# One layer of S5, grouped-query attention and experts: the order of VectorE and ScalarE between the unit loop and the last stage's square root, by hand before, the scheduler's after

## The chip, the core and the metric

The kernel runs on one core of one Trainium2 chip. The metric is the device time of one execution in microseconds (us), launch to end. The core's engines are TensorE (PE; its weight loads are a row of their own, PEld), VectorE (DVE), ScalarE (ACT), GpSimd (POOL) and SyncE (SP), beside 16 DMA engines that carry all loads. Each engine works through its own list of instructions in order, and waits on semaphores for data of the others.

## What is computed

One layer of a hybrid backbone over 256 latent tokens and 256 context tokens of width 1024, in float32. The reference, cut to what matters here:

```python
h  = _modulate(_rmsnorm(x, norm1_g), sh1, sc1)            # latent tokens
hc = _modulate(_rmsnorm(ctx, norm1_g), sh1c, sc1c)        # context tokens
proj, proj_c = h @ w_in, hc @ w_in[:, :COL_Q]             # S5 input | K | V | Q | gates
y_ssm  = _s5_mixer(proj[:, :512], proj_c[:, :512], ...)   # bidirectional scan, 32 groups
o_attn = _attention(q, k_all, v_all)                      # 8 heads of 64, 512 keys
s = gelu(y_ssm); s = s * sigmoid(s @ w_glu + b_glu)
merged = gates[:1024] * (s @ w_ssm_out) + gates[1024:] * (o_attn @ w_attn_out)
x_mix  = x + g1 * (merged @ w_out)
h2 = _modulate(_rmsnorm(x_mix, norm2_g), sh2, sc2)
out = _rmsnorm(x_mix + g2 * _moe(h2, ...), final_norm_g)  # top 4 of 32 experts
```

The modulation vectors (sh1 to g2) are products of the conditioning vector with w_mod. An expert is act(x @ w_gate_up + b_gate_up) @ w_down + b_down, with a clamped SwiGLU. All 32 experts' weights, 12 MB each, are read once.

## The kernel before

SBUF is cut into 24 pages of 1 MB (128 partitions x 2048 floats). Weights come as whole pages through SyncE's queue, in an order written out in the program; a page that becomes free is handed to the next load by `release` (L168) or `used` (L189), and since SyncE's instructions stay in program order (`load`, L104), a load whose page is not free holds up all later loads. GpSimd issues a few small DMAs of its own.

The front of the program runs up to the end of the branches: modulation, normalisation, products with w_in for the S5 input, K, V and Q, tables for the S5 kernels (`v_tables`, `w_tables`), and then **the unit loop** (16 units, from L1203). In one unit stand: half a gate tile's product (`gate_mm`, from tile 2 on with weights split into a high and a low part, `gate_split`), in some units a modulation tile's product (`mod_tile`, eight matmuls of 512 columns), two S5 kernel groups (`k_kernel`, units 2 to 5), a few steps of the scan (`scan_some`), and one softmax block (`attn`: scores, maximum, exponential; two units later the transposes; every fourth the product with V). At fixed units: `q_T` and `k_T` (unit 2: transposes of q and k, copied out by both engines); write and reading back of the S5 kernel tables through a DRAM tile Rd by GpSimd (unit 5); `mod_rows` (unit 10: modulation rows 1 and 2, kept in page 3); `scan_out` (end of unit 10: the scan's states to page 8, four ACT and four DVE copies); `shift_logits` (unit 11: transposes of a modulation row, copied to shT, which a product for the router's constant uses); readout, gelu and glu in units 12 to 15. `bias_steps` casts the expert biases b_gate_up and b_down, in page 3's rows, into bf16 parts in page 7, ACT and DVE in turn; a step stands at places from unit 9 on.

Behind the loop `branch` (L1267) multiplies by w_ssm_out (four products of 24 matmuls) and w_attn_out (four more). Each splits the next piece of weights (`wsplit`: ACT copies the high part, DVE subtracts for the low part), takes up to four bias steps, and merges with the gate on DVE. Then come `warm(AF.Sqrt, ...)`, which loads the square root's table on ACT, the output product (`out_mm`, `out_add`), the router, and 32 experts, each of eight pages of w_gate_up and four of w_down.

What sets the order: `keep_in_program_order` pins an instruction among the pinned ones of its engine, and the scheduler places the others by its own reckoning. TensorE is pinned through `pinned`, SyncE always. VectorE and ScalarE are written as `V` and `S`, objects of the class `Pinned`, whose calls are all recorded at one line, L49, and which pin while `strict["vec"]` holds. Before, it holds from ahead of the first products with w_in to the end. GpSimd is not pinned.

In the order rows below, pg_N is page N - 60 (pg_63 is page 3), pg_1242 and pg_1243 are the high and low parts of split weights (pages 13 and 10), pg_308 and pg_309 those of activations, bk_N is a bank that TensorE writes, smx and ssum are the softmax's maximum and sum.

Of the kernel before, what the change touches and what calls it, by code (L numbers as in the profile page):

```python
# [33 lines left out]
def hybrid_block(ctx: ExitStack, tc: tile.TileContext, a: dict, out: bass.AP):  # L34
# [3 lines left out]
    strict = {"on": False, "vec": False}  # L38
# [35 lines left out]
    def sm(shape, name, dt=F32):  # L74
        return pool.tile(shape, dt, name=name)
# [30 lines left out]
    def load_g(dst, src):  # L106
        return G.dma_start(dst, src)
# [95 lines left out]
    def mod_tile(reload=True):  # L203
        i, k = divmod(mods["done"], 8)
        mods["done"] += 1
        if k == 0:
            mbk[i + 1] = bank(("mod", i + 1))
        p_ = where["mod", i, k]
        for q in range(4):
            mm(mbk[i + 1][32 * q:32 * q + 32], scond[:, k], pg(p_, 512 * q, 512), k == 0, k == 7)  # L210
        if reload:
            mod_load(p_)
        return p_
# [87 lines left out]
    def warm(func, src):  # L301
        pa_(S.activation(sm([128, 1], f"warm{state['warm']}"), src, func))
        state["warm"] += 1
# [519 lines left out]
    def rope_q():  # L823
        for t in range(2):
            qv = qn[:, t].rearrange("p (h f) -> p h f", h=8)
            rope_norm(qv, q_ps[t].rearrange("p (h f) -> p h f", h=8), cosq[:, t], sinq[:, t],
                      rsn[:, 8 * t:8 * t + 8], 8, qv)
            del held["q", t]
# [17 lines left out]
    def q_split():  # L846
        for t in range(2):
            split(qn[:, t].rearrange("p (h f) -> p h f", h=8), qs[:, t, :, 0], qs[:, t, :, 1], V)
# [63 lines left out]
    def scan_some(cols):  # L912
        while cols > 0:
            step = next(scan_left, None)
            if step is None:
                return
            cols -= step[1] + 2
# [41 lines left out]
    def gate_mm(i, j):  # L959
        if j == 0:  # L960
            gbk[0] = bank("g")
        for k in range(8):
            o = gbk[0][:, 256 * j:256 * j + 256]
            if i < N_WHOLE:
                mm(o, loaded["gate", i][:, k, 128 * j:128 * j + 128], hT[1][:, k], k == 0, k == 7)
            else:
                mm3(o, wg[0][:, j, k], wg[1][:, j, k], hH[:, k], hL[:, k], k == 0, k == 7)
        if i < N_WHOLE and j:
            used("gate", i)

        if j:
            S.activation(gtl[i // 4][:, 512 * (i % 4):512 * (i % 4) + 512], gbk[0], AF.Tanh, scale=0.5)
            del held["g"]
# [15 lines left out]
    def k_kernel(g8):  # L989

        g4, g1, e = g8 // 4, g8 % 4, g8 % 2
        if g1 == 0:
            kb[0], kb[1] = bank("kf"), bank("kb")
        bf, bb = kb[0], kb[1]
        bd = bf[:, 448:512]
        for kind in range(3):
            for r, W in ((0, WR), (1, WI)):
                for q in range(4):
                    g = 8 * q + g8
                    Wq = W[q][:, g8]  # L1000
                    st = BBf[:, r, (g - e) * 16:(g - e) * 16 + 32]
                    rows_ = slice(32 * q, 32 * q + 32)
                    if kind == 0:
                        mm(bf[rows_, 112 * g1:112 * g1 + 112], st[0:64], Wq[0:64, 0:7], r == 0, r == 1)
                    elif kind == 1:
                        mm(bb[rows_, 112 * g1:112 * g1 + 112], st[64:128], Wq[64:128, 1:8], r == 0, r == 1)
                    else:
                        mm(bd[rows_, 16 * g1:16 * g1 + 16], st, CT[:, r, g], r == 0, r == 1)
        if g1 == 3:
            gs = slice(4 * g4, 4 * g4 + 4)  # L1010
            S.activation(R[:, gs, 128:240], bf[:, 0:448].rearrange("p (g m) -> p g m", g=4), AF.Copy)
            S.activation(R[:, gs, 0:112], bb[:, 0:448].rearrange("p (g m) -> p g m", g=4), AF.Copy)
            V.tensor_add(R[:, gs, 112:128], bd.rearrange("p (g m) -> p g m", g=4), Dm[:, gs])
            del held["kf"], held["kb"]
# [68 lines left out]
    def attn_norm(c_i):  # L1083
        if 0 <= c_i < 16:
            score_norm(c_i)
# [109 lines left out]
    def next_split(u, part):  # L1195
        if 2 * N_WHOLE <= u < 16:
            gate_split(u // 2, u % 2, part)
            if part and u % 2:
                used("gate", u // 2)


    n_attn = 0
    for u in range(16):  # L1203
        next_split(u + 1, 0)
        attn_norm(n_attn - 1)
        next_split(u + 1, 1)
        if u > 2:
            scan_some(P_SC)
        gate_mm(u // 2, u % 2)
        if u < 3 or (u % 2 == 0 and mods["done"] < 16):  # L1210
            mod_tile(u > 1)
        if 2 <= u < 6:
            k_kernel(2 * u - 4)
            k_kernel(2 * u - 3)
        if u == 0:
            rope_q()
        if u == 1:
            rope_k()
            q_split()
            S.activation(hH.bitcast(F32R), hT[1], AF.Copy)  # L1220
        if u == P_QT:
            for i in range(2):
                q_T(i)
                k_T(i)
            V.tensor_sub(hL.bitcast(F32R), hT[1], hH)
        if u > 1:
            scan_some(P_SC)
        if u == 4:
            mod_bias()
        if u == 5:  # L1230
            Rd = dpool.tile([16, 32, 240], F32, name="Rd")
            for q in range(4):
                for e in range(2):
                    load_g(Rd[:, 8 * q:8 * q + 8].rearrange("p (g e) m -> p e g m", e=2)[:, e],
                           R[32 * q + 16 * e:32 * q + 16 * e + 16].rearrange("p (g e) m -> p e g m", e=2)[:, e])
            kernel_in()
        if u == P_M:
            mod_rows(1)
            mod_rows(2)
        if u == P_M + 1:  # L1240
            shift_logits()
        if u >= P_B:
            next(bias_left, None)
        if u >= P_A:
            attn(n_attn)
            n_attn += 1
        if u >= P_B:
            next(bias_left, None)
        if u == P_S:
            scan_some(1000)  # L1250
            scan_out()
        if u in (P_RO, P_RO + 1):
            readout(u - P_RO)
        if u == P_RO + 1:
            release(18, 19, 11, 12)
            load(n2row, w("norm2_g")[None, :].to_broadcast([128, 1024]))
        if u == P_RT:
            readout_T()
            gelu()
        if u == 15:  # L1260
            wsplit()
            wsplit()
        if u == P_GL:
            glu()
# [172 lines left out]
    def gather_out(p, half, pb):  # L1437
        pv_(V.tensor_add(xg[p % 2][:, 4 * half:4 * half + 4], pb.rearrange("p (k m) -> p k m", k=4),
                         shk[:, 4 * half:4 * half + 4].unsqueeze(2).to_broadcast([128, 4, 128])))

    warm(AF.Sqrt, ssum[:, 15:16])
    out_mm(0, 0)
    out_mm(0, 1)
# [345 lines left out]
```

## Time and profile before

| what | us |
|---|---|
| median of 3 runs | 1308.1 |
| lowest and highest | 1303.62, 1309.07 |
| the profiled execution | 1309.45 |
| its span, first to last instruction | 1307.7 |
| TensorE busy in it | 1180.8 |
| VectorE, ScalarE, GpSimd busy | 401.4, 191.3, 43.2 |

The span's slices are 32.7 us each, and a digit there is the busy share in tenths. A row of the timeline gives the start, the busy time, the engine, the line and operation, the output and inputs, a count, and in brackets how long the engine had stood idle before it and what released it. With one line for all of VectorE's and ScalarE's work, tiles and shapes tell the operations apart.

### The profile page before, as it was taken

Reading aid. Unit: us, or ns where it says so; the run is one execution under the profiler, and the core shown is the slowest. Engines: PE = TensorE matmul, PEld = TensorE weight load, DVE = VectorE, ACT = ScalarE, POOL = GpSimd, SP = SyncE. Lnnn points to the kernel's source line nnn. Section 1 sums busy time; section 2 is a strip of 40 time slices with the busy share of each in tenths; the row PEclk is TensorE's granted clock in tenths of the full one; section 3 lists DMA queues with packets and bytes.
Section 4 is the critical chain, followed back from the end, with each engine's and each line's share of the span. In section 5 each row is a group of like instructions: output and inputs, shape, how many; then the busy total and the mean of one; then the engine's idle time right before and its main releaser. Section 6 shows DMA issues by size and latency. Waiting matters only on the chain.

```text
span 1307.7 us, 16152 instructions
## 1 busy us (share of the span) xinstructions
PE 1180.8 (90%) x6759; PEld 543.2 (42%) x6760; DVE 401.4 (31%) x869; ACT 191.3 (15%) x358; POOL 43.2 (3%) x69
## 2 busy tenths in 40 slices
PE   3999866887989999999999999989898989899986
PEld 2775655766733333333333333323232323233224
DVE  4897776465321211112111112111121111111111
ACT  3141335552111000000000000000000000000001
POOL 1200130011000000000000000000000000000000
PEclk9999987998989999999999999999999999999999
DMA  8957385666789999999999999999999999999996
GB/s 275 315 173 249 98 187 99 212 236 246 281 340 418 416 418 418 416 418 418 417 417 417 416 416 417 417 417 417 417 417 418 418 417 417 417 417 416 416 391 201
DMA packets 119134, 462.54 MB, mean 354 GB/s; under 512 B 20669, under 2 KB 42345, under 8 KB 84242
## 3 DMA queue, kind: packets, MB, share of 16 engines
q1 hardware_dynamic: 117570, 458.31, 89.2%
q0 software_dynamic: 1440, 3.15, 1.4%
q8 instruction: 55, 0.90, 0.3%
q14 instruction: 21, 0.17, 0.0%
q10 hardware_dynamic: 48, 0.01, 0.0%
HBM read 459.89 MB, written 1.54 MB: 353 GB/s over the span
## 4 chain that ended last, share of the span: by engine, by line
PE 56%; DMA 32%; DVE 6%; ACT 3%; issue 2%; SPq 1%; POOL 0%; ACTq 0%; DVEq 0%; POOLq 0%
PE bk L97 53%; DMA pg<-in_w_gate_up_dram 28%; DVE pg L49 5%; PE bk L100 3%; ACT pg L49 3%; DMA pg<-in_w_mod_dram 2%; DMA pg<-in_w_down_dram 2%; SPq L104 1%; DMA pg<-in_b_down_dram 0%; DMA pg<-in_w_out_dram 0%; DVE smx L49 0%; ACT L49 0%; DVE rsn_t L49 0%; DVE rs_t L49 0%; DVE gate L49 0%
## 5 line engine op out<-in xcount | busy, mean ns | idle before, releaser
L97 PE MATMUL bk<-pg,pg 128*64 128x512 f32 (+6 forms) x5424 | 1012.4, 473 | 68.8 <-DMA pg<-in_w_down_dram 27.9
L97 PEld LDWEIGHTS bk<-pg,pg 128*64 128x64 f32 (+3 forms) x5424 | 454.5, 152 | 567.4 <-issue 360.4
L49 ACT ACTIVATE pg<-bk 128x512 f32<-128x512 f32 (+4 forms) x154 | 76.4, 522 | 753.1 <-PE bk L100 677.9
L49 DVE TENSOR_SCALAR pg<-bk 128x512 f32<-128x512 f32 x64 | 44.3, 692 | 295.0 <-PE bk L97 295.0
L49 DVE TENSOR_TENSOR pg<-pg,pg 128x1024 f32<-128x1024 f32 (+8 forms) x136 | 118.9, 901 | 46.3 <-ACT pg L49 44.5
L49 ACT ACTIVATE pg<-pg 128x512 f32<-128x512 f32 (+9 forms) x112 | 75.6, 695 | 245.8 <-DVE pg L49 233.1
L49 DVE TENSOR_TENSOR pg<-bk,shT 128x512 f32<-128x512 f32 x32 | 22.1, 692 | 270.6 <-PE bk L97 270.6
L49 DVE TENSOR_TENSOR pg<-bk,pg 128x512 f32<-128x512 f32 (+4 forms) x52 | 32.1, 619 | 225.9 <-PE bk L97 222.3
L100 PE MATMUL bk<-ident,pg 128*128 128x128 f32 x448 | 73.6, 294 | 17.0 <-DVE cmx L49 6.1
L100 PEld LDWEIGHTS bk<-ident,pg 128*128 128x128 f32 x448 | 51.3, 146 | 78.7 <-issue 42.4
L97 PE MATMUL bk<-pg 64*128 64x512 f32 (+1 forms) x368 | 70.3, 484 | 0.0
L97 PEld LDWEIGHTS bk<-pg 64*128 64x128 f32 (+1 forms) x368 | 19.9, 159 | 50.0 <-issue 50.0
L49 DVE TENSOR_TENSOR pg<-pg 128x512 f32<-128x512 f32 (+3 forms) x89 | 37.4, 434 | 3.9 <-ACT pg L49 3.2
L97 PE MATMUL bk<-pg,selB 128*64 128x512 bf16 (+1 forms) x196 | 34.4, 388 | 0.0
L97 PE MATMUL bk<-pg,scond 128*32 128x256 f32 (+1 forms) x256 | 27.8, 532 | 7.2 <-DMA pg<-in_w_mod_dram 7.2
L49 DVE SCALAR_TENSOR_TENSOR pg<-pg 128x512 f32<-128x512 f32 (+3 forms) x67 | 30.3, 459 | 6.3 <-DMA pg<-in_x_dram 4.5
L1643 POOL DMA_DIRECT2D pg<-g2d x2 | 1.3, 640 | 899.3 <-PE bk L97 899.3
L49 DVE TENSOR_SCALAR pg<-iot,posp,gate 128x128 f32<-128x128 f32 x64 | 18.9, 340 | 0.0
L49 ACT ACTIVATE pg<-bk,smx 128x512 f32<-128x512 f32 x16 | 11.0, 686 | 42.5 <-DVE smx L49 42.4
L49 DVE COPY pg<-bk 128x512 f32<-128x512 f32 (+1 forms) x24 | 14.5, 612 | 5.8 <-PE bk L100 3.8
L49 DVE TENSOR_SCALAR pg<-iot,posp,rs 128x64 f32<-128x64 f32 x64 | 15.7, 308 | 0.1
L49 DVE TENSOR_TENSOR pg<-pg,LS 128x64 f32<-128x64 f32 (+4 forms) x36 | 15.6, 472 | 0.4
(148 smaller groups left out, 179.3 us busy)
## 6 DMA issues: line engine op xcount, KB each, us to landing
pg<-in_w_gate_up_dram SPq DMA_DIRECT2D x256, 1024.0 KB, 19.9
pg<-in_w_down_dram SPq DMA_DIRECT2D x127, 1024.0 KB, 20.0
pg<-in_w_mod_dram SPq DMA_DIRECT2D x16, 1024.0 KB, 5.9
pg<-in_w_in_dram SPq DMA_DIRECT2D x13, 1024.0 KB, 7.6
pg<-in_w_mod_dram SPq DMA_DIRECT2D x16, 512.0 KB, 9.2
pg<-in_w_out_dram SPq DMA_DIRECT2D x4, 1024.0 KB, 8.2
pg<-Rd POOLq DMA_DIRECT2D x16, 128.0 KB, 12.2
pg<-in_w_ssm_out_dram SPq DMA_DIRECT2D x2, 1024.0 KB, 5.1
```

The source lines that it names most:

```text
L49: i = f(*ar, **kw)
L97: pinned(T.matmul(*ar, **kw))
L100: pinned(T.transpose(*ar))
L104: return tc.keep_in_program_order(SP.dma_start(dst, src))
L1643: G.dma_start(late["g2"][:, 512 * j:512 * j + 512], g2d[j:j + 1].to_broadcast([128, 512]))
```

## The change

Two lines:

```diff
@@ -1200,6 +1200,7 @@
     n_attn = 0
+    strict["vec"] = False
     for u in range(16):
         next_split(u + 1, 0)
         attn_norm(n_attn - 1)
@@ -1438,6 +1439,7 @@
+    strict["vec"] = True
     warm(AF.Sqrt, ssum[:, 15:16])
     out_mm(0, 0)
     out_mm(0, 1)
```

No instruction is added or removed. The orders of TensorE, SyncE and (but for two memsets) GpSimd are the same as before. VectorE's and ScalarE's instructions from the unit loop to the square root's table load are placed by the scheduler, and some of them go ahead of the loop, among the table products of the start. Three places:

VectorE, unit 2, around the copies of the transposed q and k (pg_1071, pg_1072). Before:

```order
L49 TENSOR_TENSOR pg_76<-pg_65,pg_76 128x8x64 x2
L49 CAST pg_1071<-bk_1207 128x4x128
L49 TENSOR_TENSOR pg_1072<-bk_1213,pg_1072 128x2x256
L49 CAST pg_1071<-bk_1226 128x4x128
L49 TENSOR_TENSOR pg_1072<-bk_1232,pg_1072 128x2x256
L49 TENSOR_TENSOR pg_309<-pg_63,pg_308 128x2048
L49 TENSOR_TENSOR pg_62<-pg_68,LS 128x1024 x2
L49 TENSOR_TENSOR pg_1243<-pg_82,pg_1242 128x512 x2
L49 TENSOR_TENSOR pg_62<-pg_62,pg_68 128x1024
```

After:

```order
L49 TENSOR_TENSOR LS<-pg_62 128x64
L49 TENSOR_TENSOR pg_1243<-pg_82,pg_1242 128x512 x4
L49 TENSOR_TENSOR pg_68<-pg_69,LS 128x512
L49 COPY pg_68<-LS 128x64
L49 TENSOR_TENSOR pg_68<-pg_68 128x512
L49 CAST pg_1071<-bk_1207 128x4x128
L49 TENSOR_TENSOR pg_1072<-bk_1213,pg_1072 128x2x256
L49 TENSOR_TENSOR pg_68<-pg_68,LS 128x512
L49 CAST pg_1071<-bk_1226 128x4x128
L49 TENSOR_TENSOR pg_68<-pg_68,LS 128x512
L49 TENSOR_TENSOR pg_1072<-bk_1232,pg_1072 128x2x256
L49 TENSOR_TENSOR pg_68<-pg_68,pg_69 128x512
```

All four subtractions for gate tile 2 (pg_82) and the last scan levels (pg_68) are now ahead of or between the copies, and the subtraction of 128x2048 is no longer here: it stands among the table products of the start.

VectorE, units 10 and 11, before the copy shT. Before:

```order
L49 TENSOR_TENSOR pg_63<-bk_664,pg_63 128x512
L49 TENSOR_TENSOR pg_63<-bk_991,pg_63 128x512
L49 TENSOR_REDUCE smx<-bk_1825 128x1
L49 COPY pg_62<-bk_1830 128x4x128
L49 TENSOR_TENSOR pg_68<-pg_68,pg_69 128x512
L49 TENSOR_TENSOR pg_69<-pg_68 128x8x64
L49 COPY pg_69<-pg_68 128x7x64
L49 COPY pg_68<-LS 64x32 x4
L49 RECIPROCAL ssum<-ssum 128x1
L49 TENSOR_TENSOR pg_1243<-pg_82,pg_1242 128x512 x2
L49 COPY shT<-bk_1879 128x4x2
```

After:

```order
L49 RECIPROCAL ssum<-ssum 128x1
L49 TENSOR_TENSOR pg_63<-pg_63,pg_67 64x512 x2
L49 TENSOR_TENSOR pg_1243<-pg_82,pg_1242 128x512
L49 TENSOR_TENSOR pg_63<-pg_63,pg_67 32x512
L49 TENSOR_REDUCE smx<-bk_1825 128x1
L49 COPY pg_62<-bk_1830 128x4x128
L49 TENSOR_TENSOR pg_1243<-pg_82,pg_1242 128x512
L49 RECIPROCAL ssum<-ssum 128x1
L49 TENSOR_TENSOR pg_63<-pg_63,pg_67 32x512
L49 TENSOR_TENSOR pg_1243<-pg_82,pg_1242 128x512
L49 COPY shT<-bk_1879 128x4x2
```

The additions for the modulation rows (bk_664, bk_991) and the scan's steps (pg_68, pg_69) are gone from here, to earlier units; bias subtractions (pg_63) have come in.

ScalarE in the same units. Before, the scan's outputs (pg_68) ahead of a gate split:

```order
L49 ACTIVATE pg_1242<-pg_83 128x512 x2
L49 ACTIVATE pg_65<-pg_65,ssum 128x512
L49 ACTIVATE pg_65,ssum<-bk_1825,smx 128x512
L49 ACTIVATE pg_67<-pg_63 128x512
L49 ACTIVATE pg_68<-pg_69 64x31x32 x4
L49 ACTIVATE pg_1242<-pg_82 128x512 x2
L49 ACTIVATE pg_65<-pg_65,ssum 128x512
L49 ACTIVATE pg_76<-bk_1795 128x512
L49 ACTIVATE pg_65,ssum<-bk_1898,smx 128x512
```

After, the scan's outputs lie some units earlier, among softmax blocks 3 to 5:

```order
L49 ACTIVATE pg_68<-pg_69 64x31x32 x2
L49 ACTIVATE pg_65,ssum<-bk_1594,smx 128x512
L49 ACTIVATE pg_1242<-pg_82 128x512
L49 ACTIVATE pg_65<-pg_65,ssum 128x512
L49 ACTIVATE pg_64<-bk_1561 128x512
L49 ACTIVATE pg_1242<-pg_82 128x512
L49 ACTIVATE pg_62<-bk_1652 128x4x128
L49 ACTIVATE pg_65,ssum<-bk_1647,smx 128x512
L49 ACTIVATE pg_68<-pg_69 64x31x32
L49 ACTIVATE pg_65<-pg_65,ssum 128x512
L49 ACTIVATE pg_1242<-pg_83 128x512 x2
L49 ACTIVATE pg_68<-pg_69 64x31x32
```

Four calls of the same form were one row before and are now three rows, spread over three units.

ScalarE at the end of the branches, up to the square root's table load. Before:

```order
L49 ACTIVATE pg_308<-bk_2432 128x256
L49 ACTIVATE pg_1242<-pg_71 128x1024
L49 ACTIVATE pg_67<-pg_63 128x512
L49 ACTIVATE pg_1242<-pg_72 128x1024
L49 ACTIVATE pg_67<-pg_63 64x512
L49 ACTIVATE pg_67<-pg_63 32x512
L49 ACTIVATE pg_1242<-pg_72 128x1024
L49 ACTIVATE pg_67<-pg_63 128x512
L49 ACTIVATE pg_67<-pg_63 64x512
L49 ACTIVATE pg_67<-pg_63 32x512
L49 ACT_TABLE_LOAD
```

After:

```order
L49 ACTIVATE pg_1242<-pg_71 128x1024
L49 ACTIVATE pg_308<-bk_2432 128x256
L49 ACTIVATE pg_1242<-pg_71 128x1024
L49 ACTIVATE pg_1242<-pg_72 128x1024 x2
L49 ACTIVATE pg_67<-pg_63 128x512 x2
L49 ACTIVATE pg_67<-pg_63 64x512 x2
L49 ACTIVATE pg_67<-pg_63 32x512 x2
L49 ACT_TABLE_LOAD
```

The bias casts (pg_67) for b_down now stand behind the last two splits of w_attn_out (pg_72); the table load is still last.

## Rows read from the trace of the kernel before

**Rows 1.** the page's slices: busy tenths, granted clock (PEclk), DMA share

```profile
PE   3999866887989999999999999989898989899986
...
PEclk9999987998989999999999999999999999999999
DMA  8957385666789999999999999999999999999996
```

**Rows 2.** the chain of waits: start, us, what

```profile
178.04 15.49 DMA pg<-in_w_mod_dram
...
689.12 19.19 DMA pg<-in_w_gate_up_dram
```

**Rows 3.** windows: stretch, length, busy by engine (PE first), clock, DMA, GB/s

```profile
140.00:320.00 180.00, 136.64 (x1370) 113.81 (x1369) 111.76 (x210) 87.06 (x151) 28.40 (x40) 0.89 0.60 174
...
200.00:220.00 20.00, 13.42 (x91) 11.56 (x89) 14.39 (x31) 9.41 (x14) 0.00 (x0) 0.83 0.68 141
...
380.00:1255.00 875.00, 832.18 (x3962) 289.09 (x3960) 150.70 (x300) 49.58 (x91) 1.28 (x2) 1.00 1.01 415
```

**Rows 4.** timeline, table products and the large subtraction

```profile
88.08 0.38 ACT L49 ACTIVATE pg<-bk 128x256 f32<-128x256 f32 x1 [3.60 <-DVE pg L49]
...
149.25 2.28 DVE L49 TENSOR_TENSOR pg<-pg,pg 128x2048 fp32r<-128x2048 f32 x1
```

**Rows 5.** timeline, unit 2: copies of q and k, next gate product

```profile
145.51 0.69 DVE L49 CAST pg<-bk 128x512 fp32r<-128x512 f32 x1 [3.04 <-PE bk L100]
...
148.64 0.69 DVE L49 TENSOR_TENSOR pg<-bk,pg 128x512 fp32r<-128x512 f32 x1 [0.78 <-ACT pg L49]
...
157.59 2.80 PE L97 MATMUL bk<-pg,pg 128*128 128x256 f32 x14 [3.85 <-DVE pg L49]
```

**Rows 6.** timeline, units 5 to 8

```profile
172.52 4.11 POOL L107 DMA_DIRECT2D Rd<-pg  x8 [16.64 <-DVE pg L49]
...
174.91 1.06 PE L97 MATMUL bk<-pg,scond 128*32 128x512 f32 x8
...
183.40 0.50 PE L97 MATMUL bk<-pg,pg 128*128 128x256 f32 x2 [2.56 <-ACT pg L49]
...
193.58 1.94 PE L97 MATMUL bk<-pg,scond 128*32 128x512 f32 x8 [6.57 <-DMA pg<-in_w_mod_dram]
```

**Rows 7.** DMA issues, 120 to 160 us: size, median us to landing

```profile
pg<-in_w_mod_dram SPq DMA_DIRECT2D x2, 1024.0 KB, 4.8
```

**Rows 8.** timeline, units 9 to 11

```profile
191.88 1.53 SPq L104 DMA_DIRECT2D pg<-in_b_gate_up_dram  x3
...
211.91 1.12 PE L100 MATMUL bk<-ident,pg 128*128 128x128 f32 x4 [4.43 <-DVE pg L49]
...
215.64 8.84 ACT L49 ACTIVATE pg<-pg 64x992 f32<-64x992 f32 x6 [1.26 <-DVE pg L49]
...
225.43 1.01 PE L97 MATMUL bk<-rw_sb,shT 128*1 128x32 f32 x16 [7.59 <-DVE shT L49]
```

**Rows 9.** DMA issues, 170 to 215 us

```profile
pg<-in_b_gate_up_dram SPq DMA_DIRECT2D x3, 128.0 KB, 18.0
```

**Rows 10.** timeline, units 14 to 16

```profile
255.51 1.10 PE L97 MATMUL bk<-pg,pg 128*128 128x256 f32 x4 [2.42 <-issue]
...
275.82 0.66 PE L100 MATMUL bk<-ident,pg 128*128 128x128 f32 x4 [2.02 <-ACT pg L49]
```

**Rows 11.** timeline, the attention branches

```profile
276.24 3.12 PE L97 MATMUL bk<-pg,pg 128*128 128x256 f32 x24
...
288.77 11.40 PE L97 MATMUL bk<-pg,pg 128*64 128x256 f32 x86 [0.55 <-DVE pg L49]
...
297.59 1.52 SPq L104 DMA_DIRECT2D pg<-in_b_down_dram  x3
...
304.07 1.58 ACT L49 ACTIVATE pg<-pg 128x512 bf16<-128x512 f32 x2 [8.15 <-DMA pg<-in_b_down_dram]
...
319.05 0.69 DVE L49 SCALAR_TENSOR_TENSOR pg<-pg,pg 128x512 f32<-128x512 f32 x1
```

## The prediction, made before the changed kernel was run

> **What bounds the kernel now.** I read the slices of the span first, then the chain, then the windows, because they split the execution into two parts that answer to different things. In the slices the DMA engines reach 9 tenths in the twelfth slice and stay there to the last but one, while TensorE's busy tenths swing between 8 and 9 [rows 1]. The window from 380 to 1255 us says the same in one row: DMA share 1.01, 415 GB/s [rows 3]. Over those 875 us the kernel is a stream of expert weights at a fixed rate, and late in the chain its long pieces are loads of w_gate_up, such as 19.19 us at 689 [rows 2]. No order of VectorE or ScalarE can shorten that. What they can do is let the stream start earlier: its loads wait for pages that the front of the kernel still reads, so each microsecond by which the front ends earlier should come off the end nearly one for one.
>
> The front therefore counts. From 140 to 320 us TensorE is busy for 136.64 of 180 us at a granted clock of 0.89, with DMA at 0.60 [rows 3]. So 43.4 us are idle there, and this is the ceiling of what the change can give besides the clock. In the same row VectorE is busy 111.76 and ScalarE 87.06: neither is full, so TensorE waits for the order of their work, not its amount. The worst stretch is 200 to 220: PE 13.42 of 20 us, clock 0.83 [rows 3].
>
> **The change, part by part.** It adds and removes no operation of weight; it frees VectorE's and ScalarE's order from the unit loop to the square root's table load. TensorE, SyncE's loads and GpSimd keep their order. I walked the new order by hand at the same TensorE points, in durations of the trace. A minus is time won; the numbers at each point are the lead so far.
>
> *Start.* One subtraction of 128x2048, 2.28 us [rows 4], now stands among VectorE's table products of the start, where ScalarE waits 3.60 us for those products [rows 4]. It costs 0 if its data are late anyway and at most 2.28; I take 1.7, since TensorE follows these products one by one.
>
> *Units 1 to 4.* The first q copy (a 0.69 us cast) began at 145.51 and the last of the four ended at 149.3 [rows 5]. Now the last scan levels of the context and the four subtractions of gate tile 2's split stand ahead or between. Anything of 128x512 here takes 0.69 [rows 5], so four subtractions and four wide scan steps are 2.8 each; the short levels, about ten of 512 down to 64 columns, I estimate at 3.5, half of that price each; the copies' own are 2.8. VectorE was free for the copies at 142.5 (145.51 less its idle 3.04 [rows 5]); with 1.2 of the start's delay it begins at 143.7 and ends at 155.6, 6 us later than before. From the last copy to TensorE's next gate product at 157.59 were 8.3 us, of which TensorE idled 3.85 [rows 5], so 4.4 were work of its own, up to 1.4 of it beside the copies, hence 4.4 to 5.8 now: the product starts at 160.0 to 161.4. I take the dearer. Lead so far: +3.7, the start's delay inside it; between 0 (the short levels cost little) and +5.
>
> *Unit 8.* The scan steps are spread, so the scan kernel's last tile, which the write of Rd waits for, is final near 178. That write, 4.11 us from 172.52 [rows 6], and the reads of Rd behind it therefore start some 6 us later, the reads near 183. In the trace of before these reads were in flight beside a modulation tile's load, which took 15.49 us [rows 2]; alone such a load takes 4.8 [rows 7]. Now that load issues near 179.1, ahead of most of the reads, and lands near 186 to 188. TensorE stood 6.57 us for it and then ran its eight products in 1.94 us where the same eight took 1.06 at 174.91 [rows 6], which is the price of the clock fallen to its lower level. TensorE would be ready at 187.0 + 3.7 - 2.6, since the wait of 2.56 for ScalarE at 183.40 [rows 6] goes with the scan steps that stood there; plus 1.06 this ends near 189.3 instead of 195.5. Lead: -6, between -6.7 and +4 (the load as slow as before).
>
> By the Trainium skill (DMA: Bandwidth & Descriptors, "Queues, rings and completion order") each DMA engine takes turns between its queues packet by packet, so a load that meets the Rd reads at all would share their rate from then on. By the page the load would land near 198.7, if both it and the w_in load before it run at half speed throughout, and this step would lose and not win; the row of 15.49 beside 4.8 agrees that company triples the time. It is the mechanism behind rival 1.
>
> *Units 10 and 11.* This is the largest gap. TensorE waits 4.43 us at 211.91 for VectorE, then 7.59 us at 225.43 for the copy shT [rows 8]. The first has the two additions that finish the modulation rows behind the scan; they now come units earlier. The second stands behind ScalarE's group of 8.84 us from 215.64 [rows 8], by the order the four scan outputs and two copies of a gate split; the outputs now run in units 6 to 8. What is late next is the landing of b_gate_up: three loads were issued at 191.88 [rows 8] with a median of 18.0 us to landing [rows 9], and the bias casts and subtractions now stand in front of shT on both engines. Their data land near 207 to 210; a pair of casts (1.58 by the pair in rows 11), five subtractions and splits of 0.69 and one softmax step of some 2 lie between landing and copy: 7.0 us. The copy then comes at 214 to 217 and not just ahead of 225.4. Lead: -8, between -11 and 0 (a landing at 218 takes all of it).
>
> *Units 14 to 16.* Weight splits move ahead of and between the gelu steps; they no longer stand in front of the glu's tanh and of p's copies, where TensorE waits 2.42 us at 255.51, 2.02 at 275.82 [rows 10] and 0.55 at 288.77 [rows 11]. I take these 5.0 whole, because smaller waits between them that go too should pay for the splits' place among the gelu steps; the bounds are 0 and 5. Lead: -13.
>
> *The attention branches.* Four products, 24 matmuls of 3.12 us each [rows 11], end the front. The second ended at 300.17 (288.77 + 11.40), the last of VectorE's merges at 319.74 (319.05 + 0.69) [rows 11]: 19.57 us. Between them ScalarE stood 8.15 us for b_down, a bias that this stage doesn't need, issued at 297.59, and only at 304.07 could it cast it [rows 11]; both last weight splits were queued behind that cast. Now the casts stand behind the splits, and the remaining chain is two products and two merges: 3.1 + 3.1 + 1.4 = 7.6. That gives 12.0, at least 8 if the splits trail the products by a buffer. The bias's casts then fall beside the output product; the last of its subtractions stands behind the first output merge. I give that 0 to 1, and it delays only the release of one page.
>
> **Sum.** -6, then -8, then -13, then -25 at the stream's start: 1309.45, the profiled execution's own time, gives 1284.5. The median of the runs shown is 1.35 lower, so I say 1283. The bounds of the terms alone (-11 or 0 in the middle, -5 or 0, -12 or -8) give 1281 to 1301.
>
> **The rivals.**
> 1. *The middle gains nothing.* b_gate_up lands 8 us later because the loads share the queue with the reads of Rd, and the bias in front of shT takes the place of the scan output. For it: 18.0 us to landing is already long [rows 9], and the step depends on data that nothing in the unit needs. Against it: the reads start later, away from the loads. Then the tail keeps its waits and only the branches' 12 remain: 1297.4, 1296 by the median.
> 2. *Nothing arrives at the end.* The front ends earlier but the first pages of the stream don't come free earlier, because the loads are issued in program order and one page is held by the bias that now comes later. For it: the loads of expert weights behind b_down have their pages released by exactly this stage. Against it: the pages that come first hold the activations and split weights, which are done earlier. 1308.
> 3. *Slower: the clock.* The free order turns few long waits into many short ones, and TensorE stays at 1.2 GHz where it now has 2.4. At 0.89 the stretch's 136.64 us are 121.6 at full clock [rows 3]. At 0.83, the level of the worst stretch [rows 3], they would be 146.5, at 0.70 173.7: +37, which with -25 ends at 1320. Below 0.75 the change loses. The Trainium skill (TensorE: Matmul & The Clock Gate, "HAM oscillation — how this bites in real kernels") says that idle gaps bring the clock down and that the work behind them pays; the 1.94 against 1.06 agrees. But by the walk the long gaps are those that go.
> 4. *More: the clock comes back.* Where the long gaps go, the products behind them run at the upper level. At 0.96 the stretch's work takes 126.7, at 1.00 121.6, a further 10 to 15: 1268 to 1273, say 1271.
>
> **How the numbers follow.** Forecast 0.52, rival 1 0.20, rival 2 0.10, rival 3 0.12, rival 4 0.06. I predict 1283. The range leaves out rival 3 and the tail of rival 4, some 0.17: 1270 to 1309. Half a per cent, 6.5 us, is about what a measurement of this kernel can tell from no change, so faster is below 1301.6 and slower above 1314.6. Forecast, rival 4 and most of rival 1 are faster: 0.75. Rival 2 and the rest of 1 are within: 0.13. Rival 3: 0.12.
>
> **What would show it.** In the profile after, from the front's end backward: the last cast of b_down should stand behind the splits, and no wait of ScalarE of 8 us for b_down ahead of a TensorE wait. The wait for shT should be under 3 us, the modulation tile's 6.57 gone, and the wait of 4.43 gone; the units' gate product after the q copies should start some 3 us later. The row from 140 to 320 should have a clock above 0.89. The stream should begin about 25 us earlier and take equally long. The prediction is wrong if the clock falls, if the wait for shT is as long with a bias cast in front of it, or if the first w_gate_up loads behind b_down issue no earlier than now.

## The result and the profile after

The changed kernel takes 1270.84 us in the median of 4 runs (1269.91 to 1273.52), the kernel before 1305.86 (4 runs, 1302.03 to 1309.07): a ratio of 0.9736 with an interval of 0.9702 to 0.9771, or 35 us. On the chip of the second set of experiments it was 1269.11 against 1306.5. The forecast was 1283 and its range 1270 to 1309: the direction was right, and some 10 us of the gain were missing from it. The result lies 0.84 us above the range's lower edge, and 1269.11 lies below it.

The slices of the changed kernel's page (they answer to [rows 1]; a slice is 31.7 us now):

```profile
PE   3999996899899999999999898989898989999886
...
PEclk9999997999899999999999999999999999999999
DMA  9957484888899999999999999999999999999996
```

The windows of the changed kernel that answer to [rows 3]; the first is 20 us shorter than there, and the last is the stream, in a window moved by 40 us:

```profile
140.00:300.00 160.00, 138.87 (x1441) 119.39 (x1441) 98.52 (x192) 86.62 (x153) 27.12 (x40) 0.95 0.75 233
...
340.00:1215.00 875.00, 832.18 (x3964) 290.10 (x3966) 151.32 (x305) 50.20 (x92) 1.28 (x2) 1.00 1.01 415
```

PE 832.18 us, DMA 1.01 and 415 GB/s are to the digit what [rows 3] has for 380 to 1255: the stream of expert weights is untouched and only starts earlier. Everything was won ahead of it.

To see where, I cut the front at the same TensorE instructions in both kernels: the first modulation tile whose products are 512 columns wide, the first such tile behind the table products, the tile of unit 2 (ahead of the copies of q and k), the tile of unit 6, the end of the tile of unit 8, the product that waits for shT, and the first product with the router's weights behind the output product. Before:

```profile
76.08:94.68 18.60, 17.76 (x289) 13.49 (x288) 18.39 (x45) 10.52 (x24) 0.00 (x0) 1.00 0.77 270
94.68:141.67 46.99, 45.86 (x257) 26.99 (x257) 36.37 (x60) 6.96 (x19) 0.00 (x0) 1.00 0.60 207
141.67:174.91 33.24, 28.34 (x524) 22.69 (x523) 24.68 (x44) 13.47 (x24) 6.52 (x11) 0.95 0.41 133
174.91:195.52 20.61, 11.25 (x78) 7.85 (x77) 15.60 (x45) 8.27 (x18) 10.09 (x19) 0.84 0.99 183
195.52:225.43 29.91, 17.90 (x110) 15.74 (x110) 18.54 (x38) 17.24 (x24) 0.56 (x1) 0.79 0.60 111
225.43:335.11 109.68, 92.59 (x725) 79.37 (x725) 56.85 (x91) 48.86 (x90) 11.23 (x10) 0.92 0.64 233
```

The changed kernel:

```profile
73.00:93.08 20.08, 18.15 (x289) 13.45 (x288) 19.84 (x47) 9.84 (x22) 0.00 (x0) 1.00 0.75 262
93.08:138.90 45.82, 45.82 (x261) 26.95 (x257) 45.23 (x79) 7.09 (x19) 0.00 (x0) 1.00 0.61 208
138.90:168.64 29.74, 26.91 (x524) 21.18 (x523) 28.81 (x75) 14.16 (x28) 5.38 (x9) 1.00 0.50 162
168.64:178.43 9.79, 9.79 (x78) 7.72 (x77) 6.78 (x16) 9.21 (x13) 7.27 (x14) 1.00 1.02 273
178.43:207.31 28.88, 14.89 (x112) 12.50 (x110) 11.74 (x23) 17.83 (x31) 4.57 (x9) 0.86 0.86 139
207.31:297.67 90.36, 86.05 (x725) 76.32 (x725) 52.19 (x85) 45.89 (x84) 9.90 (x10) 0.95 0.76 277
```

The second number of a row is the length, the third TensorE's busy time, the last three the granted clock, the DMA share and GB/s. Row by row, with the prediction's terms beside them:

| stretch | before | changed | difference | predicted |
|---|---|---|---|---|
| table products | 18.60 | 20.08 | +1.5 | +1.7 |
| to the tile of unit 2 | 46.99 | 45.82 | -1.2 | +2.0 for this and the next |
| to the tile of unit 6 | 33.24 | 29.74 | -3.5 | |
| to the end of unit 8's tile | 20.61 | 9.79 | -10.8 | -9.7 |
| to the wait for shT | 29.91 | 28.88 | -1.0 | -2.0 |
| to the router's first product | 109.68 | 90.36 | -19.3 | -17.0 |
| sum | 259.03 | 224.67 | -34.4 | -25.0 |

By kind the 34.4 us are two parts. TensorE's idle time fell from 45.3 to 23.1 us, by 22.3 before rounding. Its busy time for the same products fell from 213.69 to 201.60, 12.1 us. Most of that is the clock, 0.79 to 0.95 in the last four stretches before and 0.86 to 1.00 now: with the busy time weighted by the granted clock in stretches of half a microsecond, the clock costs 15.0 us before and 4.4 now, so 10.6 are the clock's and 1.5 are other busy time. Another 3.1 us by which the profile after is ahead lie before the first row of the table, and they aren't the change's (last section).

### The profile page after: what moved, and what is told of

It is laid out like the page before. It is cut to its first block, busy times and chain, and to the rows that moved or that the text cites. A ratio compares the mean times of both kernels' runs of the same rounds, so it can differ in the third digit from the quotient of the medians.

```text
span 1269.6 us, 16157 instructions
## 1 busy us (share of the span) xinstructions
PE 1164.9 (92%) x6759; PEld 532.9 (42%) x6760; DVE 395.5 (31%) x869; ACT 191.9 (15%) x358; POOL 41.8 (3%) x69
## 4 chain that ended last, share of the span: by engine, by line
PE 57%; DMA 32%; DVE 6%; issue 2%; ACT 2%; SPq 1%; POOL 0%; DVEq 0%; ACTq 0%; POOLq 0%
PE bk L97 54%; DMA pg<-in_w_gate_up_dram 28%; DVE pg L49 5%; PE bk L100 2%; DMA pg<-in_w_down_dram 2%; DMA pg<-in_b_gate_up_dram 2%; ACT pg L49 1%; SPq L104 1%; DMA pg<-in_w_in_dram 0%; DVE LS L49 0%; DVE smx L49 0%; ACT L49 0%; DVE rs_t L49 0%; DVE gate L49 0%; DVE gs__2634 L49 0%
## 5 line engine op out<-in xcount | busy, mean ns | idle before, releaser
L97 PE MATMUL bk<-pg,pg 128*64 128x512 f32 (+6 forms) x5424 | 998.7, 470 | 55.0 <-DMA pg<-in_w_down_dram 28.5
L97 PEld LDWEIGHTS bk<-pg,pg 128*64 128x64 f32 (+3 forms) x5424 | 445.0, 150 | 548.6 <-issue 360.4
L49 DVE TENSOR_TENSOR pg<-pg,pg 128x1024 f32<-128x1024 f32 (+9 forms) x136 | 117.8, 891 | 25.6 <-ACT pg L49 24.4
L100 PE MATMUL bk<-ident,pg 128*128 128x128 f32 x448 | 72.8, 290 | 10.6 <-DVE cmx L49 6.1
L97 PEld LDWEIGHTS <-selB 128*64 128x64 bf16 x196 | 9.0, 108 | 16.1 <-issue 15.9
```

The source lines that it names most:

```text
L49: i = f(*ar, **kw)
L97: pinned(T.matmul(*ar, **kw))
L100: pinned(T.transpose(*ar))
```

## The experiments

Each kernel was timed in three rounds beside the kernel before on its chip, whose medians were 1307.5, 1306.5 and 1306.0 us in the three sets.

### The tail alone

The loop stays pinned; the switch stands behind it:

```diff
+    strict["vec"] = False
     gs = []
     for c_i in range(n_attn, 17 + LAG):
```

> VectorE and ScalarE are left to the scheduler only behind the unit loop (last softmax blocks, eight branches); the loop keeps the order laid out by hand. Theory (the gains of the loop and of the tail add, each microsecond of the front counts one for one at the end): the tail's share of the change, 17 to 19 us, so 1287 to 1290 against 1306 of the kernel before. Rival (the tail only gains where the loop has already delivered b_down's load and the pages earlier): 5 us or less, 1301 or more.

1289.18 us against 1307.52, ratio 0.9857 (0.9834 to 0.988): 18.3 us. The tail needs nothing of the loop, and its gain reaches the end whole.

### The loop alone

The switch as in the change, and back to pinned ahead of `gs = []`.

> The scheduler orders VectorE and ScalarE in the unit loop only; from the loop's end on the hand's order is back. Theory: the loop's share, 15 us, so about 1291; ScalarE again stands some 8 us for b_down between the weight splits. Rival (what the loop wins is lost again at the wait for b_down, which is set by its load and not by the loop): under 6 us, 1300 or more.

1289.68 us, ratio 0.9855 (0.9834 to 0.9876): 17.8 us. The two halves make 36.2, the change 35.0 to 37.4: they add, and the rival, that one half's lead would be lost in the other, falls.

### One queueing alone: b_down behind the splits

The kernel before, in the hand's order, with this edit in `branch`:

```diff
-        for _ in range(4):
+        for _ in range(0 if key == "attn" else 3 if i == 3 else 4):
             next(bias_left, None)
```

> The kernel before, all in the hand's order, with one edit: the casts and subtractions of b_down stand behind the eighth branch instead of between the last weight splits. Theory (this one queueing is what the branches lose): 12 us, the prediction's own term, so about 1294. Rival (in the tail the free order wins by many small moves): 4 us or less, 1302 or more.

1295.81 us, ratio 0.9919 (0.99 to 0.9939): 11.7 us, the prediction's term of 12.0. TensorE's timeline of the kernel before has these rows behind that of 288.77 in [rows 11]:

```profile
305.70 0.80 PE L97 MATMUL bk<-pg,pg 128*128 128x256 f32 x2 [5.53 <-ACT pg L49]
...
318.47 1.13 PE L97 MATMUL bk<-pg,pg 128*128 128x256 f32 x4 [1.33 <-DVE pg L49]
```

With the edit the whole stretch, from the last product with V into the output product, is one row with none of these waits:

```profile
286.21 24.07 PE L97 MATMUL bk<-pg,pg 128*64 128x256 f32 x166 [0.55 <-DVE pg L49]
```

and ScalarE's, where the cast of b_down still waits for its landing, but with nothing queued behind it that TensorE needs:

```profile
301.76 0.63 ACT L49 ACTIVATE pg<-pg 128x512 bf16<-128x512 f32 x1 [3.18 <-DMA pg<-in_b_down_dram]
```

From that product to the router's first it takes 34.79 us instead of 46.34, so the rows show 11.6 us in this place. Of the tail's 18.3 us it is the larger part, and it could have been had in the hand's order with a line.

### The first units alone

The kernel before, with the switch off in units 0 to 4 only:

```diff
     for u in range(16):
+        strict["vec"] = u > 4
```

> VectorE and ScalarE are left to the scheduler only in units 0 to 4 of the loop (what it lifts ahead of the loop included); all else is in the hand's order. Theory (the first units gain, against the prediction's loss of 3.7 us, since scan steps and the gate split go into VectorE's idle time ahead of the copies of q and k): TensorE's product of the modulation tile in unit 5 stands 3 to 5 us earlier counted from the first such tile, the large subtraction's 1.5 us included; but the modulation tile's load and the scan outputs take it back, so 0 to 3 us at the end, 1303 to 1306. Rival (as predicted, the copies come later): 2 to 4 us later there, and 1308 or more.

1301.42 us against 1306.0, ratio 0.9962 (0.9948 to 0.9976): 4.6 us. From the first 512-wide modulation tile to that of unit 6 (the expectation calls it unit 5) it takes 94.58 us, where the kernel before takes 98.83 and the changed one 95.64. The other profiles agree: the five with these units in the hand's order have 98.83 to 100.13, the nine with them free 94.58 to 97.50. The prediction's sign is wrong here. And my expectation was too careful: the waits for the tile's load, for the modulation rows and for shT are all still there, only smaller or as long as before:

```profile
184.87 1.94 PE L97 MATMUL bk<-pg,scond 128*32 128x512 f32 x8 [5.96 <-DMA pg<-in_w_mod_dram]
...
203.20 1.11 PE L100 MATMUL bk<-ident,pg 128*128 128x128 f32 x4 [4.21 <-DVE pg L49]
216.71 1.01 PE L97 MATMUL bk<-rw_sb,shT 128*1 128x32 f32 x16 [7.37 <-DVE shT L49]
```

(6.57, 4.43 and 7.59 in [rows 6, 8]). What they wait for moves forward with the first units, the issue of loads included, so the lead goes through them.

### The later units alone

```diff
     for u in range(16):
+        strict["vec"] = u < 5
```

and pinned again behind the loop.

> VectorE and ScalarE are left to the scheduler only in units 5 to 15; the first units and the tail are in the hand's order. Theory (the middle's gain is the scan, its outputs and the modulation rows spread over earlier units, and needs nothing of the first units): 9 to 12 us, 1295 to 1298. Rival (the scan can only be out of the way by unit 8 if its context part was done before unit 5): 5 us or less, 1302 or more.

1293.7 us, ratio 0.9909 (0.9884 to 0.9935): 12.3 us. With the first units' 4.6 that is 16.9 of the loop's 17.8. The scan doesn't need the early units to be out of the way in time. From the first 512-wide modulation tile to the product that waits for shT its profile has 137.92 us, where the kernel before has 149.35: 11.4 us. The prediction's lead went from +3.7 ahead of unit 8 to -8 at shT, 11.7 us.

### Bias casts behind shT

In the changed kernel the longest wait of the front is again the one for shT, now behind a bias cast. ScalarE, VectorE and TensorE between 178 and 208, and the DMA issues of 165 to 212 (they answer to [rows 8, 9]):

```profile
178.95 1.58 SPq L104 DMA_DIRECT2D pg<-in_b_gate_up_dram  x3
...
200.22 4.27 ACT L49 ACTIVATE pg<-pg 128x512 bf16<-128x512 f32 x7 [10.60 <-DMA pg<-in_b_gate_up_dram]
200.88 2.74 DVE L49 TENSOR_TENSOR pg<-pg,pg 64x512 f32<-64x512 f32 x4 [12.78 <-ACT pg L49]
...
207.31 1.01 PE L97 MATMUL bk<-rw_sb,shT 128*1 128x32 f32 x16 [12.68 <-DVE shT L49]
```

```profile
pg<-in_b_gate_up_dram SPq DMA_DIRECT2D x3, 128.0 KB, 20.0
```

TensorE waits 12.68 us, more than the 7.59 before. The experiment pins the first half of the casts behind shT's copy and behind the exponential of that unit, without moving the load:

```diff
         if u == P_M + 1:
+            strict["vec"] = True
             shift_logits()
-        if u >= P_B:
+            strict["vec"] = False
+        strict["vec"] = True
+        for _ in range(0 if u < P_B or u in (10, 11) else 2 if u in (12, 13) else 1):
             next(bias_left, None)
+        strict["vec"] = False
         if u >= P_A:
+            strict["vec"] = u == 11
             attn(n_attn)
+            strict["vec"] = False
             n_attn += 1
...
```

The bias steps behind `attn` get the same lines.

> The changed kernel, with the casts and subtractions of the first half of b_gate_up pinned behind the copy shT and the exponential of that unit; the load stays where it is. Theory (shT waits 12.68 us in the changed kernel only because both engines stand for b_gate_up in front of it): TensorE's wait there falls under 3 us and 8 to 10 us of it reach the end, about 1261 against 1271. Rival (the wait moves: the bias is then late for the second load in its page, or the next gate splits take its place): within 3 us of the changed kernel, 1268 or more.

1266.96 us, ratio 0.9689 (0.9673 to 0.9705). The changed kernel was not run beside it; its medians elsewhere are 2 and 4 us higher, but its runs there, 1264.7 to 1273.63, take in all four of these (1265.9 to 1269.68), so a gain isn't shown. The theory's 1261 falls: the wait for shT is still 8.10 us, and ScalarE now stands for another load.

```profile
201.38 1.15 ACT L49 ACTIVATE pg<-pg 128x512 fp32r<-128x512 f32 x2 [8.97 <-DMA pg<-in_w_in_dram]
```

That is a gate tile of 1 MB, issued at 181.34 in this kernel, just ahead of b_gate_up: both loads take some 20 us. So the bias's place alone is not the cause; the next experiment asks what makes both loads late.

### The reads of Rd behind the loads

The sixteen reads of Rd on GpSimd's queue run in this time. In the kernel before they started ahead of the modulation tile's load of [rows 2], which took 15.49 us:

```profile
176.94 5.00 POOL L107 DMA_DIRECT2D pg<-Rd  x9 [0.32 <-PE bk L97]
177.59 0.37 SPq L104 DMA_DIRECT2D pg<-in_w_in_dram  x1
178.04 0.53 SPq L104 DMA_DIRECT2D pg<-in_w_mod_dram  x1
```

In the changed kernel, behind it:

```profile
165.70 0.37 SPq L104 DMA_DIRECT2D pg<-in_w_in_dram  x1
...
167.43 4.10 POOL L107 DMA_DIRECT2D Rd<-pg  x8 [14.38 <-DVE pg L49]
...
169.77 0.34 SPq L104 DMA_DIRECT2D pg<-in_w_mod_dram  x1
...
172.61 3.34 POOL L107 DMA_DIRECT2D pg<-Rd  x6 [1.08 <-PE bk L97]
...
177.37 1.06 PE L97 MATMUL bk<-pg,scond 128*32 128x512 f32 x8
```

The modulation tile was issued 2.8 us ahead of the first read and TensorE doesn't wait for it, where it was issued 1.1 us behind it. b_gate_up, at 178.95, was issued in the midst of the reads. The edit lets SyncE issue the reads, behind b_gate_up in its queue:

```diff
-                load_g(Kt[hf][16 * i:16 * i + 16],
+                load(Kt[hf][16 * i:16 * i + 16],
...
         if u >= P_B:
             next(bias_left, None)
+        if u == P_B:
+            kernel_in()
```

and the call of `kernel_in` in unit 5 goes. In the changed kernel:

> The changed kernel, with the sixteen reads of Rd issued by SyncE behind the first three loads of b_gate_up (unit 9) instead of by GpSimd from unit 6 on. Theory (the loads of unit 8 to 10 take 18 to 20 us because they share the DMA engines with these reads): b_gate_up lands within 8 us of its issue, the wait for shT falls from 12.68 us to under 3, and about 10 us reach the end: 1260 to 1262 against 1271. Rival (b_gate_up takes 18 to 20 us by its own shape, or the readout now waits for the reads): 1268 or more.

1259.52 us against 1306.5, ratio 0.965 (0.9634 to 0.9667), some 10 us less than the changed kernel on the same chip (1269.11). DMA issues of 165 to 215 us, and TensorE at shT:

```profile
pg<-in_w_in_dram SPq DMA_DIRECT2D x3, 1024.0 KB, 5.5
pg<-Rd SPq DMA_DIRECT2D x16, 128.0 KB, 8.2
...
pg<-in_b_gate_up_dram SPq DMA_DIRECT2D x3, 128.0 KB, 6.2
```

```profile
196.32 0.63 PE L97 MATMUL bk<-rw_sb,shT 128*1 128x32 f32 x16 [1.97 <-DVE shT L49]
```

The landing falls from 20.0 to 6.2 us and the wait from 12.68 to 1.97. This shows that the reads made the loads late. The edit changes two things, the reads' place and their queue, and no run parts them. But the reads fill the DMA engines from either queue: in the changed kernel's profile, from 177 to 184 us, their share is 1.05 at 157 GB/s, and in this one, from 185 to 194.8 us, with the reads in SyncE's queue, 1.26 at 126 GB/s, where the stream of weights has 415. These rows speak for the place. It is the mechanism of rival 1, though what the loads and reads share is the DMA engines and not a queue (SPq and POOLq in the rows above). By the Trainium skill (DMA: Bandwidth & Descriptors, "Queues, rings and completion order") a DMA engine takes turns between the queues that have work for it, packet by packet. The 20.0 against 6.2 agrees with that.

With the reads beside the loads the time also varies more: the changed kernel's four runs on this chip go from 1264.7 to 1273.63, these four from 1259.44 to 1260.51.

The same edit in the kernel before, all in the hand's order:

> The same edit on the kernel before, all in the hand's order. Theory (the 6.57 us wait for the modulation tile and the cold products behind it come from the reads of Rd alone, not from VectorE's order): that wait goes, and TensorE is some 9 us earlier behind that tile; part of it is lost again at the scan in front of shT, so 3 to 8 us at the end, 1299 to 1304 against 1307. Rival (the load would be late for another reason, its page or the queue in front of it): the wait stays, 1306 to 1308.

1303.9 us, ratio 0.9977 (0.9964 to 0.9991): 2.6 us, less than the 3 that I had expected at the least. The wait for the modulation tile is gone and its products run in 1.06 us, as the theory says; but:

```profile
207.09 1.12 PE L100 MATMUL bk<-ident,pg 128*128 128x128 f32 x4 [7.91 <-DVE pg L49]
220.62 1.01 PE L97 MATMUL bk<-rw_sb,shT 128*1 128x32 f32 x16 [7.20 <-DVE shT L49]
```

The next wait for VectorE grew from 4.43 to 7.91 and that for shT stayed. With the scan in the hand's place, VectorE comes to the modulation rows when it does, whatever TensorE does before. So the 10.8 us of unit 8 are not the load's alone. That they could be kept because the new order had moved the scan and the modulation rows too follows from these waits; no run shows it singly.

### The large subtraction back, and the changed kernel again

> The changed kernel, with the one subtraction of 128x2048 pinned, so that it stands behind the copies of q and k again. Theory (it costs the start 1.5 to 1.7 us, and unit 2 has room for it): 1 to 1.5 us less, about 1270. Rival (in unit 2 it delays the first softmax block and the scan by its 2.3 us): the same or 1 to 2 us more.

The line is pinned by switching `strict["vec"]` on around it. 1268.92 us (1271.76, 1259.54, 1267.6 and 1270.24), ratio 0.9696 (0.9657 to 0.9736); the changed kernel beside it:

> The changed kernel itself beside the other three on the same chip: 1269 to 1273. Its profile tells how much of the first 40 us differs between executions of one order: by the theory up to 3 us, and nothing of it is the change's.

1269.11 us (1264.7 to 1273.63), ratio 0.971 (0.9682 to 0.9739). No difference at the end. From the first tile to the next behind the table products it takes 18.33 us instead of 20.08, so the start's term of 1.5 to 1.7 is right. Where it is lost again isn't settled: at the start of unit 8's tile this profile lies between the changed kernel's two (105.59 us behind the first tile, against 104.37 and 106.57). TensorE then waits 2.97 us for ScalarE, and at shT 11.64 us with a landing of 23.0. One of the four runs, 1259.54, is as fast as the kernel with the reads moved; it has no trace, and why is not known. I tried the subtraction once more without the wait for the landing.

### All of it together

The reads behind b_gate_up, and the subtraction back:

> The changed kernel with both edits that looked right: the reads of Rd behind b_gate_up on SyncE's queue, and the large subtraction back behind the copies of q and k. Theory (with the landing out of the way the start's 1.5 us reach the end, which they could not while shT waited for a load): 1257 to 1259 against 1259.5 with the first edit alone. Rival: the same 1259 to 1261.

1259.18 us, ratio 0.9649 (0.9624 to 0.9674). The same and the bias casts behind shT:

> The same, and the bias casts pinned behind shT as well. Theory (shT waits 1.97 us for them once the reads are out of the way): 1 to 2 us less, 1256 to 1258. Rival (other work takes their place): the same as without.

1258.62 us (1256.42 to 1260.19), ratio 0.9641 (0.9613 to 0.9669). Neither differs from 1259.52, measured on another chip, by more than the runs of one kernel do. With the subtraction in unit 2, TensorE waits for ScalarE some units later, 3.59 us where the changed kernel has 0.35 and the one with only the reads moved 0.32:

```profile
187.56 5.02 PE L97 MATMUL bk<-pg,pg 128*128 128x256 f32 x26 [3.59 <-ACT pg L49]
```

So the place that the scheduler gave the subtraction costs nothing that these runs can tell. The reads' edit is the one that pays, and all three kernels beat both the kernel before and the changed one.

## Why the prediction was right, and where it was not

**The bound and the conversion** held. The stream is the same and each microsecond of the front arrived: -34.4 by the table, -35.0 by the medians, and the parts timed singly add up (4.6 + 12.3 + 18.3 = 35.2, on two chips). Rival 2 falls with it: the w_gate_up loads behind b_down are issued from 272.16 us on, not from 299.15. The prediction misread one slice: DMA stays at 9 from the thirteenth on, not the twelfth, and nothing rests on it.

That 1270.84 lies inside the range is in part luck: 9.4 us of the gain were missing from the sum, and the range just reached that far.

**Start:** +1.7 predicted, +1.5 measured, and shown by the subtraction put back.

**Units 1 to 4** is the step that failed: +2.0 for these units by themselves, -4.7 measured up to the tile of unit 6. At the point that the prediction named, the gate product behind the copies, TensorE stands 80.19 us behind the first modulation tile instead of 81.51: 1.3 us earlier, the start's delay included, and not 3.7 later. I had queued the four gate subtractions and the scan levels one behind the other from the time when VectorE was free. The changed kernel's rows show them ahead of that:

```profile
140.20 2.50 DVE L49 TENSOR_TENSOR pg<-pg,pg 128x512 fp32r<-128x512 f32 x4 [0.27 <-ACT pg L49]
...
143.95 0.68 DVE L49 CAST pg<-bk 128x512 fp32r<-128x512 f32 x1
...
146.94 0.69 DVE L49 TENSOR_TENSOR pg<-bk,pg 128x512 fp32r<-128x512 f32 x1
...
153.19 3.13 PE L97 MATMUL bk<-pg,pg 128*128 128x256 f32 x24 [1.49 <-DVE pg L49]
```

Counted from the first modulation tile, the last copy ends at 74.6 us, where it was 73.3 before and I had said 79.5. I let the new work begin at 142.5, where VectorE's own list ran out ahead of the copies ([rows 5]: idle for 3.04 us), and left out the idle time that it had before. In the second row of the tables, ahead of the tile of unit 2, VectorE is busy for 36.37 of 46.99 us before and for 45.23 of 45.82 in the changed kernel. The short scan levels and scan steps went into that hole, the four subtractions stood ahead of the copies, and so less work was left between the copies and the gate product: it waits 1.49 us instead of 3.85. What ends its wait is in both traces the addition of Dm on VectorE (157.32 to 157.54 before, 152.92 to 153.13 now), which stands behind that work in the queue, and not the gate subtractions themselves.

**Unit 8:** -9.7 predicted, -10.8 measured, and the mechanism, a load ahead of the reads instead of behind, is what the rows show. The reason that I gave for it was only half of it: I had the last tile of Rd final near 178, so that the reads come some 6 us later. Counted at TensorE's tile of unit 6 the write started 1.2 us later than before (167.43 and 168.64, against 172.52 and 174.91 in [rows 6]) and the first read 1.9 us later. The other half is the load itself, which went out 2.0 us earlier by the same count. In front of it on SyncE's queue stands a gate tile's load, which waits for VectorE's subtractions of the tile before: it went out at 165.70 and not at 177.59, so the modulation tile's could follow as soon as TensorE had left its page, at 169.77. Nor would the term stand alone, as the experiment in the hand's order shows.

**Units 10 and 11** failed by the prediction's own sign: it is wrong, it says, if the wait for shT is as long with a bias cast in front of it, and the wait is 12.68 us, with bias casts in front, where it should have been under 3. The term of -2.0 against -1.0 measured came out near by luck, the wrong lead against the wrong wait. The bias in front of shT did take the place of the scan outputs, and the copy came 6.9 us behind the landing (7.0 predicted). By the prediction's clock the landing was at 207 to 210; it was at 200, with TensorE 15 us ahead rather than 8. Rival 1's mechanism was thus real: 12.68 us of wait, of which some 10 could be had back. It didn't take all of the middle's gain, which is why the rival's time, 1296, was wrong.

**Units 14 to 16 and the branches:** -17 predicted, -19.3 measured, of which b_down's place 11.7. Their rows (they answer to [rows 10, 11]):

```profile
239.03 9.29 PE L97 MATMUL bk<-pg,pg 128*128 128x256 f32 x34 [3.71 <-issue]
...
251.90 0.66 PE L100 MATMUL bk<-ident,pg 128*128 128x128 f32 x4
...
270.54 1.57 SPq L104 DMA_DIRECT2D pg<-in_b_down_dram  x3
277.13 16.71 PE L97 MATMUL bk<-pg,pg 128*128 128x256 f32 x86 [0.36 <-DVE pg L49]
277.47 1.15 ACT L49 ACTIVATE pg<-pg 128x512 bf16<-128x512 f32 x2 [2.84 <-DMA pg<-in_b_down_dram]
280.79 0.69 DVE L49 SCALAR_TENSOR_TENSOR pg<-pg,pg 128x512 f32<-128x512 f32 x1
```

The last branch and the output product are one row, 277.13 on. ScalarE waits for b_down 2.84 us, and TensorE doesn't wait for ScalarE there. Of the three waits that I took whole, 2.02 and 0.55 went, but 2.42 became 3.71. By the rows of the two windows the stretch's 19.3 us are 12.8 of idle time (17.1 to 4.3) and 6.5 of busy time at a higher clock (0.92 to 0.95), where I had put all 17 down as waits.

**The clock** was counted too low. I put in 0.9 us of it, at unit 8's tile, and made the rest a rival of its own with a chance of 0.06. But it was no case apart: in this front the gaps went and the products behind them ran at a higher clock, and 10.6 of the 34.4 us are that. Rival 4's time, 1271, is what was measured, and its price of 10 to 15 for the clock fits the 10.6: what came is rival 4 rather than the forecast. By place, the first units make 6.7 of the 9.4 us that the sum lacked; by kind, nearly all of it is the clock, 0.9 put in and 10.6 measured, while the 24.1 us of waits in the sum came to 23.8 of idle and other busy time. These are two counts of the same time and don't add. Rival 3, a lower clock from many short waits, fell: no stretch of the table has a lower clock than before. By the Trainium skill (TensorE: Matmul & The Clock Gate, "HAM oscillation — how this bites in real kernels") idle gaps bring the clock down and the work behind them pays. The table agrees in the rows where most idle time went, the third, fourth and sixth: their clock rose from 0.95, 0.84 and 0.92 to 1.00, 1.00 and 0.95. In the fifth the clock rose too, from 0.79 to 0.86, with 2.0 us more of idle time, nearly all of it now in the one wait at the row's end. I should have put this into the sum by the rows' own 1.94 against 1.06, and not only into a rival.

**Open:** why the free order's tail gains 6.6 us besides b_down's place (18.3 less 11.7) was not tried piece by piece. The rows show where: from shT to the last product with V the kernel with the free tail takes 56.80 us instead of 63.34, with 5.1 us idle instead of 9.3 and 51.7 busy instead of 54.0. Behind that product it takes 34.67, as with b_down alone moved (34.79).

## What to carry to other kernels

An engine's order is read by who waits behind its head: one place of the hand's order, a cast that waits for a load in front of weight splits, cost 11.7 us, a third of what the free order won, and one line gave it back. When work is moved ahead of something, lay it first into the engine's idle time before that point and only then queue it, and take the clock's share of each gap that closes into the sum. A transfer that the changed order newly waits for is the next thing to look at: who shares the DMA engines with it in that time was worth another 10 us.

## What was not expected

The first 70 us of the execution vary from one to the next, though TensorE's instructions and their order are the same in all: the first 512-wide modulation tile stands between 70.45 and 76.08 us in the fourteen profiles, the latest being that of the kernel before. Some 3 us of this are the clock. The sixteen matmuls behind the first wait, in the profiles of the kernel before, of the changed kernel and of the kernel with the free tail (its order is the hand's up to there):

```profile
32.80 6.67 PE L97 MATMUL bk<-pg,pg 128*128 128x256 f32 x16 [1.43 <-ACT pg L49]
```

```profile
32.71 3.69 PE L97 MATMUL bk<-pg,pg 128*128 128x256 f32 x16 [1.43 <-ACT pg L49]
```

```profile
31.39 5.17 PE L97 MATMUL bk<-pg,pg 128*128 128x256 f32 x16 [1.43 <-ACT pg L49]
```

The granted clock over these rows is 0.55, 1.00 and 0.71, so the profiled execution of the kernel before ran nearly all of this stretch at the lower level and that of the changed kernel all of it at the upper, and 6.67 times 0.55 is 3.67, the time at the upper level. Part of the distance between two single profiles can be this, and a comparison should start behind it, as the table does.
